# Smaller routing steps on VectorE and 512-column products for the third stage's units, in a two-layer encoder trunk with product-key experts

## The chip, the cores and the metric

The kernel runs on one core of one Trainium2 chip. The metric is the device time of one execution in microseconds (us). The profile names the engines PE (TensorE matmuls), PEld (TensorE weight loads), DVE (VectorE), ACT (ScalarE), POOL (GpSimd) and SP (SyncE, which issues the DMAs).

## The reference, cut to what matters

256 tokens of 1024 features go through two layers. Each layer is an attention (differential in layer 0, stick-breaking in layer 1), a layer norm, a PEER channel mixer and a layer norm. Nearly all of the time is the mixer's:

```python
def _peer(x, w_pq, sub_keys, u, v):              # xt: 256 tokens x 1024
    q = (xt @ w_pq).reshape(T, 8, 2, 64)
    scores = einsum('thcd,hckd->thck', q, sub_keys)        # 8 heads, 2 halves, 128 keys
    s_top, i_top = top_k(scores, 16)
    cand = s_top[:, :, 0, :, None] + s_top[:, :, 1, None, :]
    cand_ids = i_top[:, :, 0, :, None] * 128 + i_top[:, :, 1, None, :]
    g_s, g_i = top_k(cand.reshape(T, 8, 256), 16)
    ids = take_along_axis(cand_ids..., g_i)                # 128 experts a token, of 16384
    gates = softmax(g_s)
    h = gelu(einsum('td,ted->te', x, u[ids]))
    out = einsum('te,ted->td', gates * h, v[ids])
```

## The kernel before, in words

The mixer is dense: the kernel computes h for all 16384 experts and all tokens, sets the gates of experts that a token did not choose to zero, and multiplies by all of v. The experts are cut into 128 *units* of 128 experts, which go in pairs. Products keep fp32 accuracy by splitting both operands: a high half (rounded by ScalarE's copy, `h`, L144) and a low half (the difference `l`, L149, on VectorE, or on GpSimd for the first `N_POOL` = 14 units of a layer). Each product is three matmuls, high x high, high x low and low x high. The activations' two halves are `xh` and `xl` (`xtiles`, L189), 8 rows of 256 tokens each. The buffers of a loaded unit (`raw`, `h`, `l`) rotate over three.

`Hidden.pair` (L807) makes h of a pair: 2 units x 8 rows x 3 matmuls of 256 columns into one PSUM tile `w`, then Gelu on ScalarE (L819). The mixer has three stages.

- First stage: the first `N_STORED` = 42 units. Beside them VectorE does the routing of both token blocks (`routing`, L677): top 16 of 128 keys (`top16`: maxima L705, indices L707, replacement L709, again L712, L714), sums of candidates (L721 to L737), top 16 of those, then indices by masks and folds (L743 to L778), the gates (L780 to L784), four transposes on TensorE, two copies on ScalarE (L791, L792) into `idxT`, and the gates' low half L793. `routing` is a generator; each `yield` claims the microseconds of the work just written down, and `yield None` ends a part. `route_all` (L829) hands out the parts of the two blocks alternately. The loop at L843 adds 0.12 (first 13 units) or 0.072 us of credit per matmul and writes routing steps until the credit is used up, so the claims set where on VectorE the low halves of the units stand between routing steps. VectorE's order is the written order there (`order_r`); the order of the other engines, and where instructions of the next stage are slipped in, is made by a planner that simulates with its own costs.
- Second stage: from `idxT` the gates of 8 tokens at a time, by masks on VectorE (L887 to L904) and products on TensorE (L914, L915), drained onto the stored units (L873, L874); beside it 26 more units (`extra`).
- Third stage: the product with v, two units of v a step, in the order 13 extra pairs, 30 fresh pairs, 21 stored pairs. The fresh pairs' h is made on the way (`make_fresh`, L931): while fresh pairs last, a step holds 48 matmuls of `Hidden.pair` and 24 matmuls of 512 columns with v (`passes`, L199).

Of the kernel before, what the change touches and what calls it, by code (L numbers as in the profile page):

```python
# [10 lines left out]
F32 = mybir.dt.float32  # L11
F32R = mybir.dt.float32r
# [4 lines left out]
AF = mybir.ActivationFunctionType  # L17
OP = mybir.AluOpType
AX = mybir.AxisListType

P = 128
D = 1024
T = 256
NB = 2
DC = 8
# [22 lines left out]
N_POOL = 14  # L48
# [10 lines left out]
def trunk(ctx: ExitStack, tc: tile.TileContext, x, xT, ln_g, ln_b, w_qkv, w_o_a, lam_p, subln, w_kv,  # L59
          w_q, w_o_b, w_pq, sub_k, uT, v, rope, ln_c, out):  # L60
    nc = tc.nc
# [4 lines left out]
    work = ctx.enter_context(tc.tile_pool(name="work", bufs=2))  # L66
    psum = ctx.enter_context(tc.tile_pool(name="psum", bufs=4, space=bass.MemoryType.PSUM))
# [3 lines left out]
    def reg(off, *shape):  # L71
        n = int(np.prod(shape))
        a = big[:, off:off + n]
        if len(shape) == 2:
            return a.rearrange("p (a b) -> p a b", b=shape[1])
        if len(shape) == 3:
            return a.rearrange("p (a b c) -> p a b c", b=shape[1], c=shape[2])
        if len(shape) == 4:
            return a.rearrange("p (a b c d) -> p a b c d", b=shape[1], c=shape[2], d=shape[3])
        return a  # L80
# [106 lines left out]
    units = Units()  # L187

    def xtiles():  # L189
        return (work.tile([P, DC, T], F32R, name="xh", bufs=1), work.tile([P, DC, T], F32R, name="xl", bufs=1))  # L190

    def accs(tag):
        a = [[psum.tile([P, 512], F32, name=tag, tag=tag) for _ in range(NB)] for _ in range(2)]
# [181 lines left out]
    def diff_attention(xh, xl):  # L375
# [161 lines left out]
        for i, _ in enumerate(v_steps(av)):  # L537
# [12 lines left out]
            if i == 7:  # L550
                s2(1)
                s3(1)
        units.later(reg(O_A, NB, D), x)
        oh, ol = xtiles()
        acc = accs("acc")
        wo = moving_steps(acc, oh, ol, lambda d: w_o_a[0, d * P:(d + 1) * P, :], tail=TAIL,
# [13 lines left out]
    def stick_breaking(xh, xl, yv, gb):  # L570
# [60 lines left out]
        for f in range(2):  # L631
            for b in range(NB):
                nc.vector.tensor_copy(V[:, b, f * 512:(f + 1) * 512], av[b][f])
        oh, ol = xtiles()
        acc = accs("acc")
        wo = moving_steps(acc, oh, ol, lambda d: w_o_b[0, d * P:(d + 1) * P, :], tail=TAIL,
# [11 lines left out]
    def peer(layer, xh, xl, spill, o_res):  # L648
# [8 lines left out]
        hx = {}  # L657
# [19 lines left out]
        def routing(b, sc):  # L677
            o = 23552 + b * 4096
            def half(off, *shape):
                n = int(np.prod(shape))  # L680
                return big[:, off:off + n // 2].bitcast(F16).rearrange(
                    "p (a b c) -> p a b c" if len(shape) == 3 else "p (a b) -> p a b",
                    **dict(zip("bc" if len(shape) == 3 else "b", shape[1:])))
# [4 lines left out]
            di = half(o + 584, HP, K, 2)  # L688
# [6 lines left out]
            ef = reg(o + 1576, 3, HP, K)  # L695
# [7 lines left out]
            def top16(lists):  # L703
                for vals, s, i in lists:
                    nc.vector.max(s[:, 0:8], vals)  # L705
                for vals, s, i in lists:
                    nc.vector.max_index(i[:, 0:8], s[:, 0:8], vals)  # L707
                for vals, s, i in lists:
                    nc.vector.match_replace(vals, s[:, 0:8], vals, -3.0e38)  # L709
                yield 0.55 * len(lists)  # L710
                for vals, s, i in lists:
                    nc.vector.max(s[:, 8:16], vals)  # L712
                for vals, s, i in lists:
                    nc.vector.max_index(i[:, 8:16], s[:, 8:16], vals)  # L714
                yield 0.55 * len(lists)

            for l0 in range(0, 2 * HP, 4):
                yield from top16([(sc[:, li, :], s16l[:, li, :], i16l[:, li, :]) for li in range(l0, l0 + 4)])
# [4 lines left out]
            nc.vector.tensor_tensor(di, ia[:, :, 1:K + 1].unsqueeze(3).to_broadcast([P, HP, K, 2]),  # L723
                                    ia[:, :, 0:K].unsqueeze(3).to_broadcast([P, HP, K, 2]), OP.subtract)
            nc.vector.tensor_copy(i2, iu[:, :, 1, :].unsqueeze(3).to_broadcast([P, HP, K, 2]))
            for a0, off, n in SPANS[:8]:
                if a0 in (6, 7):
                    continue
                if a0 == 5:
                    nc.vector.tensor_tensor(  # L730
                        cs[:, :, off:off + 6].rearrange("p h (a b) -> p h a b", b=2),
                        s16[:, :, 0, 5:8].unsqueeze(3).to_broadcast([P, HP, 3, 2]),
                        s16[:, :, 1, 0:2].unsqueeze(2).to_broadcast([P, HP, 3, 2]), OP.add)
                    continue
                nc.vector.tensor_tensor(cs[:, :, off:off + n], s16[:, :, 1, 0:n],
                                        s16[:, :, 0, a0:a0 + 1].to_broadcast([P, HP, n]), OP.add)
            nc.vector.tensor_tensor(cs[:, :, NCAND - 8:NCAND], s16[:, :, 0, 8:16],  # L737
                                    s16[:, :, 1, 0:1].to_broadcast([P, HP, 8]), OP.add)
            yield 2.0
            for h0 in range(0, HP, 4):  # L740
                yield from top16([(cs[:, h, :], g16[:, h, :], p16u[:, h, :]) for h in range(h0, h0 + 4)])
            yield None
# [2 lines left out]
            def fold(dst):  # L745
                w = K // 2
                while w > 1:
                    nc.vector.tensor_tensor(prd[:, :, 0:w, :], prd[:, :, 0:w, :], prd[:, :, w:2 * w, :], OP.add)
                    w //= 2
                nc.vector.tensor_tensor(dst, prd[:, :, 0, :], prd[:, :, 1, :], OP.add)  # L750

            def each(t):
                return t.unsqueeze(1).to_broadcast([P, HP, K, K])

            def times(t):
                nc.vector.tensor_tensor(
                    prd.rearrange("p h a (k t) -> p (h a) k t", t=2), stp.rearrange("p h a (k t) -> p (h a) k t", t=2),
                    t.rearrange("p h a t -> p (h a) t").unsqueeze(2).to_broadcast([P, HP * K, K // 2, 2]), OP.mult)

            nc.vector.tensor_tensor(stp, p16h.unsqueeze(2).to_broadcast([P, HP, K, K]), each(off16), OP.is_ge)  # L760
            nc.vector.tensor_tensor(prd, stp, each(len16), OP.mult)
            yield 2.4
            fold(cc)
            nc.vector.tensor_tensor(cc, p16h, cc, OP.subtract)
            yield 1.6
            times(di)
            fold(ef[:, 0])
            yield 2.6
            nc.vector.tensor_tensor(stp, cc.unsqueeze(2).to_broadcast([P, HP, K, K]), each(row16), OP.is_equal)
            times(i2)  # L770
            fold(ef[:, 1])
            yield 3.8
            ef = ef.rearrange("p c h k -> p c (h k)")
            ei = i16.rearrange("p h c k -> p (h c k)").bitcast(I32).rearrange("p (c n) -> p c n", c=2)
            nc.vector.tensor_copy(ei[:, 1], ef[:, 1])
            nc.vector.tensor_scalar(ei[:, 0], ei[:, 1], 4, None, OP.logical_shift_right)
            nc.vector.tensor_scalar(ei[:, 1], ei[:, 1], 15, None, OP.bitwise_and)
            nc.vector.tensor_copy(ef[:, 1:3], ei)  # L778
            gx = s16.rearrange("p h c k -> p (h c k)")[:, 0:P].rearrange("p (h k) -> p h k", k=K)
            nc.vector.tensor_tensor(gx, g16, g16[:, :, 0:1].to_broadcast([P, HP, K]), OP.subtract)  # L780
            nc.scalar.activation(gx, gx, AF.Exp)
            nc.vector.tensor_reduce(sm[:, 0, :], gx, axis=AX.X, op=OP.add)
            nc.vector.reciprocal(sm[:, 1, :], sm[:, 0, :])
            nc.vector.tensor_tensor(gx, gx, sm[:, 1, :].unsqueeze(2).to_broadcast([P, HP, K]), OP.mult)  # L784
            yield 2.0
            pt = psum.tile([P, 4, P], F32, name="acc", tag="acc")
            for c in range(3):
                nc.tensor.transpose(pt[:, c, :], ef[:, c, :], ident)
# [1 line left out]
            bs = slice(b * P, (b + 1) * P)  # L790
            nc.scalar.activation(idxT[:, 0:3, bs], pt[:, 0:3, :], AF.Copy)  # L791
            nc.scalar.activation(idxT[:, 3, bs], pt[:, 3, :], AF.Copy, scale=GS)  # L792
            nc.vector.scalar_tensor_tensor(idxT[:, 4, bs], pt[:, 3, :], GS, idxT[:, 3, bs], OP.mult, OP.subtract)  # L793
            yield 0.5

        class Hidden:
# [10 lines left out]
            def pair(self, i, dst):  # L807
# [10 lines left out]
                            yield i + k  # L818
                nc.scalar.activation(dst, ps.rearrange("p a b -> p (a b)"), AF.Gelu)  # L819

        hidden = Hidden()

        def slot(i):
            return big[:, i * T:(i + 2) * T]
# [3 lines left out]

        def route_all():  # L829
            rs = [routing(b, sc[b]) for b in range(NB)]  # L830
            for r in rs:
                yield from iter(lambda r=r: next(r), None)
            for r in rs:
                yield from iter(lambda r=r: next(r), None)
            for r in rs:
                yield from r

        side = route_all()
        credit = 0.0
# [2 lines left out]
        hidden.fetch()  # L842
        for i in range(0, N_STORED, 2):  # L843
            for u in hidden.pair(i, slot(i)):
                credit += 0.12 if u + 1 < N_POOL else 0.072
                while credit > 0.0:
                    c = next(side, None)
                    if c is None:
                        credit = -1e9
                        break  # L850
                    credit -= c
# [40 lines left out]
        for t8 in range(0, T, 8):  # L892
            if t8 % (2 * NR) == 0:
                parts(t8)
            rs = slice(t8 // 2 % NR, t8 // 2 % NR + 4)
# [13 lines left out]
            for r in range(2):  # L909
                ps = psum.tile([P, 4, NE], F32, name="acc", tag="acc")  # L910
# [20 lines left out]
        def make_fresh():  # L931
            if fq:
                i = fq.pop(0)
                hx[i] = work.tile([P, 2 * T], F32, name="hx", tag="hw", bufs=RING)
                for _ in hidden.pair(i, hx[i]):
                    pass

        wq = {}

# [28 lines left out]
        for s in range(n + 1):  # L968
            if s >= len(ext) - 2:
                make_fresh()  # L970
            if s >= 1:
                i = order[s - 1]
# [26 lines left out]
    xh, xl = xtiles()  # L999
# [26 lines left out]
    for layer in range(2):  # L1026
        acc = diff_attention(xh, xl) if layer == 0 else stick_breaking(xh, xl, reg(res, NB, D), gb)
        xh, xl = xtiles()
# [5 lines left out]
        if layer == 0:  # L1034
            xh, xl = xtiles()
# [48 lines left out]
```

## Time and profile before

| what | us |
|---|---|
| median of 3 runs (lowest, highest) | 1892.78 (1888.84, 1894.35) |
| the profiled execution, whole | 1894.14 |
| its span, first to last instruction | 1892.3 |

The span of the trace is 1.8 us shorter than the time of the execution that it belongs to. Times in rows are counted from the span's start. Busy times of matmuls overlap, since matmuls are pipelined, so the mean duration of one is longer than the distance between two starts. "Idle before" is the engine's idle time just ahead of an instruction, with what released it.

### The profile page before, as it was taken

What the parts mean: (1) busy time and instruction counts of PE and PEld (TensorE: products, weight loads), DVE (VectorE), ACT (ScalarE), POOL (GpSimd) and SP (SyncE); (2) the same over time, 40 slices, a digit from 0 to 9 for tenths busy, and PEclk for the clock granted to TensorE, in tenths of its full rate; (3) what the DMA queues carried; (4) which work ended last, traced back from release to release, by engine and by line L of the source; (5) the groups of instructions that cost most, each with busy time, mean ns of one, the idle gap of its engine ahead of it and who ended that gap; (6) DMA issues with size and microseconds to landing.
All of it is one profiled execution on the core that took longest, in us unless ns stands there. A gap on an engine that the chain in (4) does not pass through costs nothing.

```text
span 1892.3 us, 30931 instructions
## 1 busy us (share of the span) xinstructions
PE 1831.4 (97%) x12264; PEld 1655.8 (87%) x12264; DVE 1232.2 (65%) x2402; ACT 911.5 (48%) x1244; POOL 176.6 (9%) x190
## 2 busy tenths in 40 slices
PE   8999989999999999999999999899999999999997
PEld 6879989898999999978798799889989999998786
DVE  5666988986555555575553569889865555555655
ACT  4545445545444444454447454454544444445442
POOL 5434200000000000000122251000000000000001
PEclk9989999999999999999999999999999999999999
DMA  6533544335555555575643345443355555555753
GB/s 210 177 134 135 184 136 137 123 124 200 179 200 191 191 186 182 186 266 190 211 152 105 123 157 179 133 146 113 134 202 184 191 181 189 185 191 192 255 190 133
DMA packets 90449, 325.40 MB, mean 172 GB/s; under 512 B 10176, under 2 KB 10560, under 8 KB 89664
## 3 DMA queue, kind: packets, MB, share of 16 engines
q1 hardware_dynamic: 90304, 323.43, 50.4%
q8 instruction: 96, 1.57, 0.3%
q14 instruction: 49, 0.40, 0.1%
HBM read 320.24 MB, written 3.15 MB: 171 GB/s over the span
## 4 chain that ended last, share of the span: by engine, by line
PE 77%; DVE 17%; DMA 2%; issue 2%; ACT 1%; POOL 1%; SPq 0%; POOLq 0%; ACTq 0%; DVEq 0%
PE acc L199 38%; PE w L816 28%; PE acc L244 4%; DVE l L149 3%; DVE gl L900 2%; DVE big L873 2%; DVE gh L900 2%; DVE oa L904 1%; PE w L244 1%; PE acc L444 1%; PE w L199 1%; DVE big L707 1%; DVE big L709 1%; DMA big<-in_ln_g 1%; DVE big L714 1%
## 5 line engine op out<-in xcount | busy, mean ns | idle before, releaser
L144 ACT ACTIVATE h<-raw 128x1024 fp32r<-128x1024 f32 x579 | 606.9, 1059 | 854.7 <-PE acc L199 457.0
L149 DVE TENSOR_TENSOR l<-raw,h 128x1024 fp32r<-128x1024 f32 x526 | 642.8, 1235 | 530.4 <-ACT h L144 530.1
L816 PE MATMUL w<-xh,l 128*128 128x256 f32 x2048 | 580.3, 285 | 15.6 <-DVE l L149 15.6
L816 PE MATMUL w<-xh,h 128*128 128x256 f32 x2048 | 586.6, 287 | 2.1 <-ACT h L144 2.1
L816 PE MATMUL w<-xl,h 128*128 128x256 f32 x2048 | 580.6, 284 | 0.0
L816 PEld LDWEIGHTS w<-xh,l 128*128 128x128 f32 x2048 | 392.8, 192 | 21.6 <-DVE l L149 16.6
L199 PE MATMUL acc<-l,wh 128*128 128x512 f32 x1024 | 399.3, 391 | 2.9 <-DVE l L149 2.9
L816 PEld LDWEIGHTS w<-xh,h 128*128 128x128 f32 x2048 | 393.8, 192 | 7.9 <-ACT h L144 2.5
L199 PE MATMUL acc<-h,wl 128*128 128x512 f32 x1024 | 399.5, 391 | 0.0
L816 PEld LDWEIGHTS w<-xl,h 128*128 128x128 f32 x2048 | 393.7, 192 | 4.8
L199 PE MATMUL acc<-h,wh 128*128 128x512 f32 x1024 | 278.3, 391 | 0.0
L199 PEld LDWEIGHTS acc<-l,wh 128*128 128x128 f32 x1024 | 192.6, 188 | 40.0 <-DVE l L149 3.8
L199 PEld LDWEIGHTS acc<-h,wl 128*128 128x128 f32 x1024 | 192.8, 188 | 36.8
L199 PEld LDWEIGHTS acc<-h,wh 128*128 128x128 f32 x1024 | 188.1, 188 | 35.6
L149 POOL TENSOR_TENSOR l<-raw,h 128x1024 fp32r<-128x1024 f32 x53 | 130.4, 2461 | 178.2 <-ACT h L144 167.4
L959 DVE TENSOR_TENSOR wl<-big,wh 128x512 fp32r<-128x512 f32 x128 | 87.0, 687 | 5.1 <-PE acc L199 4.7
L173 POOL TENSOR_TENSOR ahead<-big,ahead 128x512 fp32r<-128x512 f32 x12 | 16.5, 1403 | 754.2 <-ACT ahead L163 754.2
L958 ACT ACTIVATE wh<-big 128x512 fp32r<-128x512 f32 x128 | 78.2, 620 | 12.1 <-PE acc L199 7.8
L915 PE MATMUL acc<-oa,gl 128*128 128x128 f16 x512 | 66.3, 220 | 14.2 <-DVE gl L900 12.7
L295 POOL TENSOR_TENSOR mv<-mv,mhalf 128x1 f32<-128x1 f32 x8 | 4.8, 600 | 745.1 <-DVE mv L294 745.1
L914 PE MATMUL acc<-oa,gh 128*128 128x128 f16 x512 | 70.6, 220 | 0.0
L874 ACT ACTIVATE big<-acc 128x344 f32<-128x344 f32 x128 | 51.4, 453 | 30.5 <-DVE big L873 30.5
(215 smaller groups left out, 1749.2 us busy)
## 6 DMA issues: line engine op xcount, KB each, us to landing
raw<-in_uT SPq DMA_DIRECT2D x256, 512.0 KB, 3.3
raw<-in_v SPq DMA_DIRECT2D x256, 512.0 KB, 3.6
raw<-in_w_qkv SPq DMA_DIRECT2D x23, 512.0 KB, 3.7
raw<-in_w_kv SPq DMA_DIRECT2D x12, 512.0 KB, 4.0
raw<-in_w_o_a SPq DMA_DIRECT2D x8, 512.0 KB, 4.0
big<-in_w_pq SPq DMA_DIRECT2D x8, 512.0 KB, 6.7
raw<-in_w_pq SPq DMA_DIRECT2D x8, 512.0 KB, 5.0
raw<-in_w_q SPq DMA_DIRECT2D x8, 512.0 KB, 3.8
```

The lines of the kernel that those rows point to most:

```text
L144: self.h = nc.scalar.activation(h, raw, AF.Copy)
L149: o = e.tensor_tensor(l, raw, h.bitcast(F32), OP.subtract)
L199: nc.tensor.matmul(acc[b][f], a[:, d, ts], w[:, fs], start=(first and q == 0), stop=(last and q == 2))
L244: nc.tensor.matmul(acc[n // 2][:, n % 2, :], w[:, c:c + P], a[:, d, :], start=(d == 0 and q == 0 and n % 2 == 0), stop=(d == DC - 1 and q ...
L816: nc.tensor.matmul(ps[:, k, :], w[:, ds], a[:, d, :], start=(d == 0 and q == 0), stop=(d == DC - 1 and q == 2))
L873: nc.vector.scalar_tensor_tensor(wv[:, 0:N_STORED], pv[:, 0:N_STORED], 1.0 / GS, wv[:, 0:N_STORED], OP.mult, OP.mult)
L874: nc.scalar.activation(wv[:, N_STORED:], pv[:, N_STORED:], AF.Copy, scale=1.0 / GS)
L900: nc.vector.tensor_tensor(dst.rearrange("p r (a b) t -> p r a b t", b=16), hi[:, rs].unsqueeze(3).to_broadcast([P, 4, 8, 16, 2]), lo[:, rs ...
L914: nc.tensor.matmul(ps[:, k, :], gh[:, m, :, e], oa[:, m, :, e], start=True, stop=False)
L915: nc.tensor.matmul(ps[:, k, :], oj[:, m, :, e], oa[:, m, :, e], start=False, stop=True)
L958: nc.scalar.activation(wh, s, AF.Copy)
L959: nc.vector.tensor_tensor(wl, s, wh.bitcast(F32), OP.subtract)
```

## The change

Four things change. (1) The two halves of the activations become one tile, `xhl`, in which the rows of high and low half alternate. (2) `top16` and the third part of the routing offer more and smaller steps, with other claims, and the credit per matmul goes from 0.12 to 0.13 and from 0.072 to 0.08. (3) L793 moves behind a `yield None`, and `route_all` has three rounds, so that the L793 of both blocks come after everything else of the routing. (4) `make_fresh` uses a new `wide_pair`: per row the high half of the unit is multiplied with both halves of the activations in one matmul of 512 columns, the low half with the high half of the activations in one of 256 columns; each unit has a PSUM tile of its own, whose two halves VectorE adds into the destination, and Gelu works in place.

```diff
     def xtiles():
-        return (work.tile([P, DC, T], F32R, name="xh", bufs=1), work.tile([P, DC, T], F32R, name="xl", bufs=1))
+        units.both = work.tile([P, DC, 2, T], F32R, name="xhl", bufs=1)
+        return units.both[:, :, 0, :], units.both[:, :, 1, :]
...
             def top16(lists):
                 for vals, s, i in lists:
                     nc.vector.max(s[:, 0:8], vals)
+                yield 0.2 * len(lists)
                 for vals, s, i in lists:
                     nc.vector.max_index(i[:, 0:8], s[:, 0:8], vals)
+                yield 0.26 * len(lists)
                 for vals, s, i in lists:
                     nc.vector.match_replace(vals, s[:, 0:8], vals, -3.0e38)
-                yield 0.55 * len(lists)
+                yield 0.26 * len(lists)
                 for vals, s, i in lists:
                     nc.vector.max(s[:, 8:16], vals)
+                yield 0.2 * len(lists)
                 for vals, s, i in lists:
                     nc.vector.max_index(i[:, 8:16], s[:, 8:16], vals)
-                yield 0.55 * len(lists)
+                yield 0.26 * len(lists)
...
             nc.vector.tensor_copy(i2, iu[:, :, 1, :].unsqueeze(3).to_broadcast([P, HP, K, 2]))
+            yield 1.2
...
-            yield 2.0
+            yield 1.2
...
             nc.vector.tensor_tensor(stp, p16h.unsqueeze(2).to_broadcast([P, HP, K, K]), each(off16), OP.is_ge)
+            yield 1.3
             nc.vector.tensor_tensor(prd, stp, each(len16), OP.mult)
-            yield 2.4
+            yield 1.2
             fold(cc)
             nc.vector.tensor_tensor(cc, p16h, cc, OP.subtract)
+            yield 1.8
+            times(di)
+            yield 1.2
+            fold(ef[:, 0])
             yield 1.6
-            times(di)
-            fold(ef[:, 0])
-            yield 2.6
             nc.vector.tensor_tensor(stp, cc.unsqueeze(2).to_broadcast([P, HP, K, K]), each(row16), OP.is_equal)
+            yield 1.2
             times(i2)
+            yield 1.2
             fold(ef[:, 1])
-            yield 3.8
+            yield 1.6
...
             nc.vector.tensor_copy(ef[:, 1:3], ei)
+            yield 0.9
...
             nc.vector.tensor_tensor(gx, gx, sm[:, 1, :].unsqueeze(2).to_broadcast([P, HP, K]), OP.mult)
-            yield 2.0
+            yield 0.8
...
             nc.scalar.activation(idxT[:, 3, bs], pt[:, 3, :], AF.Copy, scale=GS)
+            yield None
             nc.vector.scalar_tensor_tensor(idxT[:, 4, bs], pt[:, 3, :], GS, idxT[:, 3, bs], OP.mult, OP.subtract)
             yield 0.5
...
+            def wide_pair(self, dst):
+                for k in range(2):
+                    if len(self.got) < 2:
+                        self.fetch()
+                    h, l = self.got.pop(0)
+                    ps = psum.tile([P, 2 * T], F32, name="w", tag="w")
+                    for d in range(DC):
+                        ds = slice(d * P, (d + 1) * P)
+                        nc.tensor.matmul(ps, h[:, ds], both[:, d].rearrange("p c t -> p (c t)"), start=(d == 0),
+                                         stop=False, skip_group_check=True)
+                        nc.tensor.matmul(ps[:, 0:T], l[:, ds], xh[:, d, :], start=False, stop=(d == DC - 1),
+                                         skip_group_check=True)
+                    nc.vector.tensor_reduce(dst[:, k * T:(k + 1) * T], ps.rearrange("p (c t) -> p t c", t=T), axis=AX.X, op=OP.add)
+                nc.scalar.activation(dst, dst, AF.Gelu)
...
         def route_all():
             rs = [routing(b, sc[b]) for b in range(NB)]
-            for r in rs:
-                yield from iter(lambda r=r: next(r), None)
-            for r in rs:
-                yield from iter(lambda r=r: next(r), None)
+            for _ in range(3):
+                for r in rs:
+                    yield from iter(lambda r=r: next(r), None)
             for r in rs:
                 yield from r
...
-                credit += 0.12 if u + 1 < N_POOL else 0.072
+                credit += 0.13 if u + 1 < N_POOL else 0.08
...
-                for _ in hidden.pair(i, hx[i]):
-                    pass
+                hidden.wide_pair(hx[i])
```

## Rows read from the trace of the kernel before

**Rows 1.** The page, part 1: busy us (share of the span) xinstructions of each engine

```profile
PE 1831.4 (97%) x12264; PEld 1655.8 (87%) x12264; DVE 1232.2 (65%) x2402; ACT 911.5 (48%) x1244; POOL 176.6 (9%) x190
```

**Rows 2.** Table by stretches of layer 0's mixer: length, PE PEld DVE ACT POOL busy, PEclk, DMA

```profile
172.00:209.00 37.00, 35.93 (x300) 35.73 (x298) 36.93 (x255) 18.28 (x21) 24.07 (x10) 1.00 0.41 143
209.00:250.00 41.00, 40.71 (x339) 40.71 (x340) 37.31 (x149) 17.09 (x21) 0.00 (x0) 1.00 0.54 183
...
266.20:282.00 15.80, 9.37 (x64) 9.35 (x64) 15.38 (x26) 3.83 (x6) 0.00 (x0) 0.78 0.29 93
282.00:302.00 20.00, 20.00 (x171) 19.88 (x170) 12.88 (x22) 11.23 (x14) 0.00 (x0) 1.00 0.53 172
302.00:420.00 118.00, 110.89 (x1141) 107.13 (x1140) 113.89 (x249) 60.36 (x106) 0.00 (x0) 1.00 0.35 121
...
475.00:806.00 331.00, 331.00 (x2122) 301.74 (x2121) 176.56 (x176) 151.91 (x178) 0.00 (x0) 1.00 0.56 188
```

**Rows 3.** The list of waits, whole span: us in total, times, longest

```profile
PE w L816 <- DVE l L149: 15.6, 4, 6.4
...
DVE hi L887 <- ACT idxT L791: 11.0, 2, 5.5
```

**Rows 4.** Timeline of PE: start, us, instruction [idle before <-releaser]

```profile
209.29 0.39 PE L816 MATMUL w<-xh,l 128*128 128x256 f32 x1 [1.36 <-DVE l L149]
...
272.64 0.58 PE L816 MATMUL w<-xh,l 128*128 128x256 f32 x1 [6.43 <-DVE l L149]
```

**Rows 5.** Timeline of DVE in layer 0's first stage

```profile
208.02 2.35 DVE L149 TENSOR_TENSOR l<-raw,h 128x1024 fp32r<-128x1024 f32 x2
...
237.38 0.22 DVE L743 CAST big<-big 128x128 f16<-128x128 uint32 x1
...
258.85 0.28 DVE L782 TENSOR_REDUCE big<-big 128x8 f32<-128x128 f32 x1 [1.62 <-ACT big L781]
...
259.62 1.22 DVE L149 TENSOR_TENSOR l<-raw,h 128x1024 fp32r<-128x1024 f32 x1
266.35 0.23 DVE L887 TENSOR_TENSOR hi<-iota,idxT 128x128 f16<-128x128 f16 x1 [5.51 <-ACT idxT L791]
...
271.37 2.36 DVE L149 TENSOR_TENSOR l<-raw,h 128x1024 fp32r<-128x1024 f32 x2
273.64 1.48 DVE L748 TENSOR_TENSOR big<-big 128x1024 f16<-128x1024 f16 x3
...
295.11 0.29 DVE L793 SCALAR_TENSOR_TENSOR idxT<-acc,idxT 128x128 f16<-128x128 f32 x1 [3.31 <-ACT idxT L792]
```

**Rows 6.** Timeline of ACT ahead of block 0's copies

```profile
262.96 1.06 ACT L144 ACTIVATE h<-raw 128x1024 fp32r<-128x1024 f32 x1 [2.03 <-PE w L816]
...
265.83 0.48 ACT L791 ACTIVATE idxT<-acc 128x384 f16<-128x384 f32 x1
```

**Rows 7.** The chain that ended last, in order of time: start, us, what

```profile
272.64 8.47 PE w L816 x48
...
426.15 48.99 PE acc L199 x216
475.14 3.59 PE w L816 x30
486.03 3.47 PE w L816 x29
...
497.28 3.47 PE w L816 x29
...
1213.86 7.36 PE w L816 x48
```

**Rows 8.** Groups of instructions, shapes apart: busy us, mean ns | idle before

```profile
L816 PE MATMUL w<-xh,h 128*128 128x256 f32 x2048 | 586.6, 287 | 2.1 <-ACT h L144 2.1
...
L819 ACT ACTIVATE hx<-w 128x512 f32<-128x512 f32 x86 | 49.9, 581 | 0.0
...
L470 DVE TENSOR_REDUCE big<-w 128x2 f32<-128x512 f32 x8 | 5.4, 688 | 4.0 <-PE w L468 4.0
```

More of the change, by code (lines that the diff above doesn't have):

```diff
@@ L819, in pair @@
                 nc.scalar.activation(dst, ps.rearrange("p a b -> p (a b)"), AF.Gelu)
+            def wide_pair(self, dst):
[12 more added lines that the diff above has]
+                nc.scalar.activation(dst, dst, AF.Gelu)
+        both = units.both
         hidden = Hidden()
```

## The prediction

> **What bounds the kernel now.** I read the page first, then the table by stretches, the list of waits, and at the stalls the timelines of TensorE, VectorE and ScalarE. TensorE has work over 97% of the span [rows 1], so a gain must be fewer TensorE cycles or one of its few gaps. The stretches of the first layer show which stage has what [rows 2]. In the third stage (475 to 806 us: 30 pairs of fresh units, each beside two units of v) TensorE is busy throughout and VectorE little more than half of it, so only TensorE's own time counts there. In the first stage it is the other way round: VectorE has 36.93 of 37 us at 172 to 209, and at 266 to 282 TensorE works 9.4 of 15.8 us with its clock granted at 0.78 on the mean, between its levels of 1.2 and 2.4 GHz. The second stage (302 to 420) has VectorE at 97%, and the diff does not touch it. The second layer repeats the pattern.
>
> The list of waits names the gaps of the first stage: TensorE waits for a unit's low half (L149 on VectorE) four times, 15.6 us [rows 3]. The first layer has one of 1.36 and one of 6.43 us [rows 4], and 2 x 7.79 = 15.6 makes the second layer's the same. How the long one comes about stands in the two timelines. VectorE ends block 0's gates, does one low half at 259.62, and then idles 5.51 us until ScalarE's copy L791 [rows 5]; that copy runs at 265.83, behind a split that began at 262.96 [rows 6]. L793, next in VectorE's written order, needs the copy's successor L792, so VectorE has to idle there; L887 of the second stage was merely slipped in front of it. The next low halves stand behind this and start at 271.37, and TensorE resumes at 272.64. The clock is low afterwards: 48 matmuls take 8.47 us there and 7.36 us in the second layer [rows 7], against 48 x 0.1197 = 5.75 us in the third stage (30 of them in 3.59 us) [rows 7].
>
> **Third stage, TensorE.** A unit has 24 matmuls of 256 columns now, and 8 of 512 and 8 of 256 after: the same columns in a third fewer instructions. Matmuls overlap, so their mean duration is no price; the chain gives start to start. A 256-column one costs 0.1197 us (3.59/30), a 512-column one with a new weight each time 0.2268 us (48.99/216) [rows 7]. Now: 24 x 0.1197 = 2.873. After: 8 x 0.2268 + 8 x 0.1197 = 2.772. That is 0.101 us a unit. The period confirms the prices: 48 x 0.1197 + 24 x 0.2268 = 11.19, and 497.28 - 486.03 = 11.25 us [rows 7]. Fresh units: 128 - 42 - 26 = 60 a layer, 120 in all, hence **-12.1 us**. The bounds are 0, should the excess over the columns not be one per instruction, and -12.1.
>
> The Trainium skill's page "TensorE: Matmul & The Clock Gate", section "Back-to-back issue gap", speaks against this size: it gives the warm isolated gap as N/2.4 plus about 2.5 ns, so that by it (an estimate) 8 matmuls fewer save 8 x 2.5 = 20 ns a unit and 2.4 us in all, not 12.1. The trace does not agree: 119.7 and 226.8 ns lie 13 ns above what that page's N/2.4 gives.
>
> **Third stage, VectorE and ScalarE.** Added are 2 reductions a pair, 120 in all, that read 128x512 out of PSUM. The nearest row is a reduction of that size from PSUM, 0.688 us [rows 8]; its output is narrower and its stride shorter, so the bounds are 0.69 and twice that. I take 0.69: 120 x 0.69 = 83 us of VectorE. It is costed at nothing because of idle time: 176.6 + 41 of 331 us [rows 2] is 66%. What stands behind a reduction is the next low halves. Three buffers rotate, so the unit three ahead gets its high half when TensorE has ended unit k: 1.06 us on ScalarE, 1.14 on VectorE and some 0.3 of hand-over make it ready 2.5 us after, and it is needed two units later, 2 x 2.87 + 0.24 = 6.0 us. The slack is 3.5 us. A reduction of unit k also waits for the end of unit k, so even one queued ahead of that low half takes 0.7 of the 3.5. Without that cover each would cost up to 0.69, 83 us in all. Gelu stays one instruction of 0.58 us [rows 8], now in place; the product that needs it comes two steps of 11 us later. PSUM tiles go from one to two a pair out of four: the pair after next finds its tiles free a whole step earlier. DMA issues keep their number and order.
>
> **Layout of the two halves.** Each row of a half stays contiguous; only the step between rows doubles. I take 0. If the shared tile made a reader of the high half wait for the low half, the first product after each of three layer norms would be some 1 us late, 3 us in all.
>
> **Routing.** Removed: VectorE's wait for L792 between block 0's gates and block 1's third part. With L793 behind both blocks, VectorE goes straight on to block 1, some 23 us of work, while the transposes and copies pass. Block 1's own wait (3.31 us at 295.11 [rows 5]) stays, with L793 of block 0 ahead of it. Gone with the stall: 2 x 6.43 + (8.47 - 5.75) + (7.36 - 5.75) = 17.2 us. Gone too, the 1.36 us twice (2.7): the low half at 208.02 stands behind a whole half list of the candidates [rows 5]. By the new steps, 13 units x 24 x 0.13 = 40.6 us of claims are handed out before it, which end after the first four maxima of that list (37.8 for both blocks' first part, then 1.2, 1.2, 0.8). Some 1.4 us of index and replace steps move behind it. Sum 19.9 us.
>
> What is late next: the new claims are handed out faster, 0.08 x 24 = 1.92 us a unit against 1.73, and one low half of 1.14 goes with each. A block's third part takes 259.62 - 237.38 = 22.2 us less six low halves (6.8), so 15.4 us, of which 1.62 is waiting for Exp [rows 5] (a low half is 1.14 start to start: two take 271.37 to 273.64); it claims 12.8 and so is spread over 6.67 units. VectorE needs 15.4 + 6.67 x 1.14 = 23.0 us for what TensorE eats in 6.67 x 2.87 = 19.1, and falls 3.9 us behind per block, 7.8 per layer, against the slack of 3.5: TensorE waits 4.3. (Before, 12.4 claimed at 1.73: 3.0 behind per block.) Bounds: 0, and 7.6 if block 1's 3.31 comes on top. The same sum of before gives block 1 a lag of 3.0 + 3.3 over 3.5, and TensorE is busy 20.00 of 20 us there [rows 2]; so it overstates, and I take 3 us a layer, in pieces too short to lower the clock (after the wait of 1.36 us it stayed at 1.00 [rows 2, 4]). **Routing: -19.9 + 6 = -14 us.** Does the second stage keep it? Its drains need all stored units, so it starts when the first stage ends on TensorE; its first sets (some 3 us of VectorE), now done in the stall, must fit into the first stage's last units, where VectorE works 12.88 of 20 us [rows 2]. They fit.
>
> **Sum.** The profiled execution took 1894.14 us (span 1892.3), 1.4 above the median of the three runs. 1894.1 - 12.1 - 14 = 1868.0, and on the median's footing **1867 us**.
>
> **Rivals.** *Another wait takes the stall's place*: the planner slips L887 or L889 in front of block 1's steps again, where they wait for block 0's copies, or the lag of 7.8 comes out in full with a low clock behind it. For it: VectorE is FIFO, and the 5.51 us were put down to L887. Against it: that idling needed L793 next in line. The routing then brings 2 us or so: 1894.1 - 12.1 - 2, 1879 on the median's footing. *A larger gain*: no lag shows at all, 1861. *The wide form saves little*, because the 13 ns hang on something else than the number of instructions: 1879 by the routing's 14 us alone. Against it: both widths show the same excess. *Slower*: the planner puts a unit's reduction ahead of the low half that TensorE needs for the very next unit. Then that low half starts only after the end of the unit before, TensorE idles 0.69 + 1.14 = 1.8 us, and all 120 times this is 220 us. It decides from 26/120 = 0.22 us a unit, or one unit in eight so queued: 1900 and more. Against it: in the third stage VectorE idles for ScalarE's split, so low halves are queued well ahead. *It does not do what it says*: the planner works from its own costs; if new orders cost in other places what is won here, the time stays within 0.3%, 1887 to 1898.
>
> **How the numbers follow.** Both parts as summed, with 0 to 7.6 us of lag a layer, 0.62 (1861 to 1876); another wait (1879) 0.16; the wide form saves little 0.10; no change 0.06; slower 0.06. I count the gain without lag into the first. 0.3% of 1893 us is 5.7 us, about what a measurement of this kernel can tell from no change (the three runs lie 5.5 apart). Faster by more than that: 0.62 + 0.16 + 0.10 = 0.88. The range goes from 1858 (no lag, and the 2.1 us in which the first stage waits for ScalarE's high half [rows 8] gone as well) to 1881 (one of the two parts wholly lost), and leaves out the last two cases and some of the edges.
>
> **What would show it.** Matmuls fall by 960 to 11304, with 960 of 512 columns into w. The period of the third stage falls from 11.25 to 11.05 us with TensorE still busy all through. 120 reductions near 0.69 us stand on VectorE; waits of TensorE for them or for low halves there would refute the cover. The wait of L887 for L791 is gone, TensorE's waits for L149 in the first stage fall from 15.6 to about 6 us, none over 3, and the granted clock is 1.00 at 260 to 285. The prediction is wrong if a wait of 5 us stays in the first stage, if a 512-column product into w costs more than 0.24 us, or if the second stage grows by what the first gave.

## The result and the profile after

The changed kernel takes 1870.88 us (median; 1868.66 to 1874.6), the kernel before beside it 1890.81. The ratio is 0.990, with a 95% interval of 0.9883 to 0.9917: faster by 19.9 us. The prediction was 1867 us with a range of 1858 to 1881.

The page of the changed kernel, part 1, answers to [rows 1]:

```profile
PE 1818.9 (97%) x11304; PEld 1598.8 (86%) x11304; DVE 1311.6 (70%) x2522; ACT 920.4 (49%) x1244; POOL 176.6 (9%) x190
```

960 matmuls are gone, and VectorE has 79 us more to do. The table by stretches, in the columns of [rows 2]; the first two lines are the end of layer 0's first stage, where the stall was, the third is the third stage:

```profile
246.00:262.50 16.50, 13.82 (x115) 13.39 (x113) 12.48 (x28) 9.69 (x12) 0.00 (x0) 1.00 0.39 125
262.50:277.00 14.50, 14.50 (x120) 14.41 (x121) 12.26 (x20) 6.42 (x7) 0.00 (x0) 1.00 0.58 180
...
464.00:800.00 336.00, 336.00 (x1688) 283.55 (x1687) 223.16 (x244) 162.00 (x186) 0.00 (x0) 1.00 0.63 191
```

The clock stays at 1.00 where it was 0.78, and TensorE is still busy all through the third stage, with VectorE at 66%. The list of waits of the changed kernel, answering to [rows 3] (us in total, times, longest):

```profile
DVE hx L844 <- PE w L842: 38.7, 84, 0.7
...
DVE big L792 <- ACT big L791: 9.9, 4, 2.7
...
PE w L827 <- DVE l L149: 5.5, 5, 2.2
```

TensorE's waits for low halves fell from 15.6 to 5.5 us. The reductions (L844) wait for TensorE, not TensorE for them. Where the time of the two profiled executions went is read best from the chain in order of time (start, us, what) at the same places of the program. Of the kernel before:

```profile
138.47 23.04 PE acc L244 x192
...
406.86 3.88 PE w L816 x32
...
1079.07 23.67 PE acc L244 x192
...
1347.23 3.88 PE w L816 x32
```

Of the changed kernel, where L245 is L244 and L827 is L816:

```profile
134.51 23.04 PE acc L245 x192
...
395.90 3.88 PE w L827 x32
...
470.33 2.78 PE acc L200 x12
...
473.45 1.84 PE acc L200 x8
...
478.33 0.94 PE acc L200 x4
...
481.82 4.56 PE acc L200 x20
...
490.96 0.93 PE acc L200 x4
...
492.58 2.78 PE acc L200 x12
...
781.87 2.78 PE acc L200 x12
...
1064.82 23.81 PE acc L245 x192
...
1326.87 3.88 PE w L827 x32
```

From the query product (first place) to a place late in the second stage (second place) the kernel before takes 268.4 us in layer 0 and 268.2 in layer 1, the changed one 261.4 and 262.1: the routing gave 7.0 + 6.1 = 13.1 us. Two steps of the third stage take 492.58 - 470.33 = 22.25 us, and the 28 steps up to 781.87 take 311.54 us, so one takes 11.126 us for 11.25 [rows 7]; 60 steps save 7.4 us.

The spans differ by 24.3 us, and 3.96 of these lie ahead of the first place (138.47 and 134.51). Most of these come from the granted clock there, not from the change. The table by stretches for layer 0's attention, first of the kernel before:

```profile
86.00:91.00 5.00, 5.00 (x25) 4.58 (x26) 3.46 (x9) 3.38 (x14) 0.00 (x0) 0.61 0.55 193
91.00:101.00 10.00, 10.00 (x49) 8.43 (x48) 5.47 (x18) 4.95 (x21) 1.03 (x1) 0.50 0.00 0
101.00:112.00 11.00, 10.83 (x69) 10.09 (x68) 7.66 (x24) 5.46 (x14) 4.45 (x50) 0.85 0.15 50
```

and of the changed one:

```profile
86.00:91.00 5.00, 5.00 (x33) 4.57 (x33) 3.81 (x10) 2.85 (x11) 0.00 (x0) 0.66 0.48 135
91.00:101.00 10.00, 10.00 (x55) 9.14 (x55) 7.46 (x25) 6.57 (x28) 3.46 (x49) 0.66 0.01 2
101.00:112.00 11.00, 10.83 (x71) 9.39 (x69) 6.05 (x17) 5.37 (x9) 4.20 (x4) 1.00 0.17 48
```

With levels of 1.0 and 0.5 of the full clock (2.4 and 1.2 GHz) the first had 5 x 0.78 + 10 + 11 x 0.3 = 17 us at the low clock, the second 5 x 0.68 + 10 x 0.68 = 10; 7 us at half speed are 3.5 us. Of the change, only the layout of the activations reaches this stretch. With the layout edit alone (below) the profiled execution had 1.00, 0.83 and 1.00 there and a span of 1886.7 us, while the median was that of the kernel before. So medians are compared below, and within traces only the same stretches.

### The profile page after: what moved, and what is told of

Read it like the earlier page. It is cut to its first block, busy times and chain, and to the rows that moved or that the text cites. A ratio compares the mean times of both kernels' runs of the same rounds, so it can differ in the third digit from the quotient of the medians.

```text
span 1868.0 us, 29132 instructions
## 1 busy us (share of the span) xinstructions
PE 1818.9 (97%) x11304; PEld 1598.8 (86%) x11304; DVE 1311.6 (70%) x2522; ACT 920.4 (49%) x1244; POOL 176.6 (9%) x190
## 4 chain that ended last, share of the span: by engine, by line
PE 80%; DVE 13%; issue 2%; DMA 2%; ACT 2%; POOL 1%; SPq 0%; ACTq 0%; POOLq 0%; DVEq 0%
PE acc L200 38%; PE w L827 12%; PE w L840 12%; PE w L842 6%; PE acc L245 4%; DVE l L149 4%; DVE gl L926 2%; DVE big L899 2%; DVE gh L926 2%; PE w L245 1%; DVE oa L930 1%; PE w L200 1%; PE acc L445 1%; DMA big<-in_ln_g 1%; ACT h L144 1%
## 5 line engine op out<-in xcount | busy, mean ns | idle before, releaser
L144 ACT ACTIVATE h<-raw 128x1024 fp32r<-128x1024 f32 x579 | 613.5, 1060 | 821.9 <-PE acc L200 333.7
L827 PE MATMUL w<-xhl,h 128*128 128x256 f32 x2176 | 400.0, 286 | 0.3 <-ACT h L144 0.2
L840 PE MATMUL w<-xhl,h 128*128 128x512 f32 x960 | 340.0, 396 | 0.0
L827 PEld LDWEIGHTS w<-xhl,h 128*128 128x128 f32 x2176 | 338.1, 192 | 0.9 <-ACT h L144 0.7
L827 PE MATMUL w<-xhl,l 128*128 128x256 f32 x1088 | 308.3, 285 | 5.7 <-DVE l L149 5.5
L842 PE MATMUL w<-xhl,l 128*128 128x256 f32 x960 | 268.8, 280 | 0.0
L840 PEld LDWEIGHTS w<-xhl,h 128*128 128x128 f32 x960 | 180.5, 188 | 42.5
L827 PEld LDWEIGHTS w<-xhl,l 128*128 128x128 f32 x1088 | 208.1, 192 | 7.6 <-DVE l L149 6.9
L842 PEld LDWEIGHTS w<-xhl,l 128*128 128x128 f32 x960 | 181.2, 189 | 6.2
L844 DVE TENSOR_REDUCE hx<-w 128x256 f32<-128x512 f32 x120 | 82.7, 690 | 38.9 <-PE w L842 38.7
L200 PE MATMUL acc<-h,xhl 128*128 128x512 f32 x256 | 84.2, 403 | 6.2 <-ACT h L132 4.8
L983 ACT ACTIVATE wh<-big 128x512 fp32r<-128x512 f32 x128 | 77.7, 616 | 15.6 <-PE acc L200 11.1
```

The source lines that it names most:

```text
L144: self.h = nc.scalar.activation(h, raw, AF.Copy)
L200: nc.tensor.matmul(acc[b][f], a[:, d, ts], w[:, fs], start=(first and q == 0), stop=(last and q == 2))
L827: nc.tensor.matmul(ps[:, k, :], w[:, ds], a[:, d, :], start=(d == 0 and q == 0), stop=(d == DC - 1 and q == 2))
L840: nc.tensor.matmul(ps, h[:, ds], both[:, d].rearrange("p c t -> p (c t)"), start=(d == 0), stop=False, skip_group_check=True)
L842: nc.tensor.matmul(ps[:, 0:T], l[:, ds], xh[:, d, :], start=False, stop=(d == DC - 1), skip_group_check=True)
L844: nc.vector.tensor_reduce(dst[:, k * T:(k + 1) * T], ps.rearrange("p (c t) -> p t c", t=T), axis=AX.X, op=OP.add)
```

## The experiments

The change was cut into its parts. Each run is given with its median and the ratio to the kernel before (median 1890.25 for the first four, 1889.7 for the next four, 1891.14 for the last two).

**L793 moved, alone.** Claims, steps and credits as before:

```diff
             nc.scalar.activation(idxT[:, 3, bs], pt[:, 3, :], AF.Copy, scale=GS)
+            yield None
             nc.vector.scalar_tensor_tensor(idxT[:, 4, bs], pt[:, 3, :], GS, idxT[:, 3, bs], OP.mult, OP.subtract)
...
-            for r in rs:
-                yield from iter(lambda r=r: next(r), None)
-            for r in rs:
-                yield from iter(lambda r=r: next(r), None)
+            for _ in range(3):
+                for r in rs:
+                    yield from iter(lambda r=r: next(r), None)
```

> The kernel before with L793 moved behind both blocks alone; claims, steps and credits as before. Theory (the stall was VectorE's wait for L792): the wait of 5.5 us and the stall of 6.43 us are gone, the waits of 1.36 us stay; the lag per block is the old 3.0 us, 6.0 for two against 3.5 of slack, so at most 2.5 us of waits come in: 11 to 15 us below the kernel before. Rival (the coarse steps made the stall): under 4 us below, with a wait of 4 us or more left.

1877.58 us, ratio 0.9928 (0.9915 to 0.9941): 12.7 us below. Its list of waits:

```profile
DVE hi L887 <- ACT idxT L791: 3.4, 2, 1.7
...
PE w L817 <- DVE l L149: 6.5, 7, 1.4
```

No wait for a low half is over 1.4 us. One moved line does what the whole routing part does. L887 is still slipped in, but costs 1.7 us and not 5.5.

**Smaller steps and new credits, alone.** The routing's edits and both credits, with L793 left where it was (the inverse of the diff above, on the changed routing):

> The kernel before with the smaller steps and the new credits alone; L793 stays behind each block's copies. Theory: the waits of 1.36 us go, the stall of 6.43 us stays or grows by the faster claims (3.9 us of lag per block for 3.0): between 3 us below the kernel before and 2 above. Rival (the coarse steps made the stall): 10 us or more below.

1890.76 us, ratio 1.0002 (0.9993 to 1.0011): nothing. Its list of waits shows the stall, now 5.7 us long. The wait of 1.36 us is gone from layer 0, but a new one of 2.94 us stands at 290.79, behind block 1's gates:

```profile
PE w L825 <- DVE l L149: 16.9, 4, 5.7
...
DVE hi L896 <- ACT idxT L800: 10.7, 2, 5.3
```

**The whole routing part, alone.** The changed kernel with `xtiles` and `make_fresh` as before:

> The kernel before with the routing's part of the change alone (steps, credits, L793 behind both blocks); third stage as before. Theory: 13 us below the kernel before, first stages 6 to 7 us shorter per layer, TensorE's waits for low halves about 3 us per layer. Rival (the wide form won 12): 8 us below.

1877.35 us, ratio 0.9933 (0.9919 to 0.9946): 12.9 us below, as with L793 alone. TensorE waits 5.3 us for low halves, longest 2.2.

**The wide form, alone.** The kernel before with `xhl` and `wide_pair`:

```diff
-                for _ in hidden.pair(i, hx[i]):
-                    pass
+                hidden.wide_pair(hx[i])
```

> The kernel before with the shared tile and wide_pair alone; the routing is as before. Theory (the wide form won 7.1 us, because 512 and 256 columns in turn cost 234 + 116 = 350 ns and not the 346.5 of the prediction): 7 us below the kernel before, and the stall of 6.43 us per layer still there. Rival (the wide form won the predicted 12 us, and the routing less): 12 us below. Rival (layout or planner give something of their own ahead of the mixer): 11 us below, with the attention shorter at the same clock.

1882.68 us, ratio 0.9960 (0.9947 to 0.9972): 7.6 us below, which excludes the 12 us of the rival (the interval is 5 to 10 us). The waits of the first stage are those of before (15.9 us, longest 6.4). The parts add: 12.9 + 7.6 = 20.5, and both together gave 19.9.

**The layout, alone.** Only `xtiles` changed:

> The kernel before with the shared tile alone, no other edit. Theory: no difference within 2 us. Rival (a reader of the high half waits for the low half, or the other step between rows costs something): 3 us or more above; or below, if the 4 us that the profiled executions differ by ahead of the first mixer are the layout's.

1889.86 us, ratio 0.9997 (0.9988 to 1.0006). The layout costs and gives nothing that can be measured.

**Each reduction twice.**

```diff
-                    nc.vector.tensor_reduce(dst[:, k * T:(k + 1) * T], ps.rearrange("p (c t) -> p t c", t=T), axis=AX.X, op=OP.add)
+                    for _ in range(2):
+                        nc.vector.tensor_reduce(dst[:, k * T:(k + 1) * T], ps.rearrange("p (c t) -> p t c", t=T), axis=AX.X, op=OP.add)
```

> The changed kernel with each of the 120 reductions done twice (same values). Theory (VectorE's idle time covers them): 83 us more of VectorE and the time within 2 us of the changed kernel, no wait of TensorE in the third stage. Rival (a reduction holds up the next low halves): 10 us or more above it.

1869.70 us, 1.2 below the changed kernel's median and within its runs. Its group of reductions (shapes, count | busy us, mean ns | idle before) and the table's line of the third stage:

```profile
L845 DVE TENSOR_REDUCE hx<-w 128x256 f32<-128x512 f32 x240 | 164.7, 687 | 36.2 <-PE w L842 35.2
```

```profile
464.00:800.00 336.00, 336.00 (x1688) 283.49 (x1687) 253.70 (x302) 162.65 (x186) 0.00 (x0) 1.00 0.61 191
```

82 us more of VectorE in all, 76% of it used in the third stage, and TensorE has no gap. The cover is real, and it holds for twice the load.

**The second credit back to 0.072.**

```diff
-                credit += 0.13 if u + 1 < N_POOL else 0.08
+                credit += 0.13 if u + 1 < N_POOL else 0.072
```

> The changed kernel with the second credit back from 0.08 to 0.072. Theory (the lag of VectorE behind the faster claims makes the remaining waits): a block's third part claims 12.8 at 1.73 us a unit, 7.41 units, 15.4 + 7.41 x 1.14 = 23.8 us of VectorE for 21.3 of TensorE, 2.5 us of lag for 3.9; the waits for low halves fall from 2.7 us per layer to under 1, and the time by 2 to 4 us. Rival (the end of the routing decides): the routing ends 4 units later, the second stage starts late, 0 to 6 us above the changed kernel.

1868.28 us, ratio 0.9890 (0.9875 to 0.9905), an interval that overlaps the changed kernel's. The theory fell: the waits for low halves did not shrink. The median is 2.6 us lower, which is what the theory forecast, but by luck: the waits that it spoke of stayed. The timeline of TensorE in layer 0's first stage, first of the changed kernel ([idle before <-releaser]):

```profile
256.90 0.39 PE L827 MATMUL w<-xhl,l 128*128 128x256 f32 x1 [0.47 <-DVE l L149]
...
262.48 0.39 PE L827 MATMUL w<-xhl,l 128*128 128x256 f32 x1 [2.21 <-DVE l L149]
...
278.34 0.33 PE L799 MATMUL acc<-ident,big 128*128 128x128 f32 x1 [0.98 <-DVE big L794]
```

and with the lower credit:

```profile
262.48 0.39 PE L827 MATMUL w<-xhl,l 128*128 128x256 f32 x1 [0.47 <-DVE l L149]
...
268.05 0.39 PE L827 MATMUL w<-xhl,l 128*128 128x256 f32 x1 [2.20 <-DVE l L149]
```

The same two waits, 5.6 us later. What made them stands in VectorE's timeline of the changed kernel:

```profile
250.53 0.29 DVE L790 TENSOR_TENSOR big<-big 128x128 f32<-128x128 f32 x1
253.46 0.28 DVE L792 TENSOR_REDUCE big<-big 128x8 f32<-128x128 f32 x1 [2.65 <-ACT big L791]
...
259.66 0.23 DVE L913 TENSOR_TENSOR hi<-iota,idxT 128x128 f16<-128x128 f16 x1 [0.96 <-ACT idxT L801]
...
261.20 1.22 DVE L149 TENSOR_TENSOR l<-raw,h 128x1024 fp32r<-128x1024 f32 x1
```

Two waits for ScalarE stand ahead of the late low half: 2.65 us for the Exp of block 0's gates, and 0.96 us for the copy L801, in front of an instruction of the second stage that the planner put between two folds. ScalarE's timeline shows what each waited behind:

```profile
251.82 1.28 ACT L791 ACT_TABLE_LOAD   x1
...
257.36 1.28 ACT L830 ACT_TABLE_LOAD   x1
...
259.15 0.48 ACT L801 ACTIVATE idxT<-acc 128x384 f16<-128x384 f32 x1
```

An ACT_TABLE_LOAD of 1.28 us stands directly ahead of the Exp (L791), and another ahead of the Gelu (L830) behind which the copy runs. That these two waits make the low half late is read from the order of the rows; no run took one of them away. The claims are not wholly without a part: the wait for the Exp was 1.62 us before [rows 5] and is 3.62 us with the lower credit. What the lower credit did remove is TensorE's wait of 0.98 us for the gates ahead of block 1's transposes. From the first to the second place of the chain, layer 0 takes 260.0 us with it for 261.4.

**512s first, then 256s.**

```diff
                     for d in range(DC):
                         ds = slice(d * P, (d + 1) * P)
                         nc.tensor.matmul(ps, h[:, ds], both[:, d].rearrange("p c t -> p (c t)"), start=(d == 0),
                                          stop=False, skip_group_check=True)
+                    for d in range(DC):
+                        ds = slice(d * P, (d + 1) * P)
                         nc.tensor.matmul(ps[:, 0:T], l[:, ds], xh[:, d, :], start=False, stop=(d == DC - 1),
                                          skip_group_check=True)
```

> The changed kernel, with wide_pair's eight products of 512 columns first and its eight of 256 after them. Theory (a 512 next to a 256 costs 3.8 ns more than the two cost among their own kind): 8 x 226.7 + 8 x 119.6 = 2.77 us a unit for 2.80, so 3.6 to 4.4 us below the changed kernel. Rival (the 512-column product into w is dear in itself, at 234 ns): no difference, and adjacent ones keep 234 ns.

1865.39 us, ratio 0.9868 (0.9853 to 0.9884): 5.5 us below the changed kernel's median, with intervals that barely touch. Its chain in order of time, in the third stage:

```profile
470.76 4.56 PE acc L200 x20
...
475.56 1.84 PE w L840 x8
477.40 0.95 PE w L844 x8
...
479.96 0.91 PE acc L200 x4
...
481.93 4.56 PE acc L200 x20
...
493.10 4.56 PE acc L200 x20
...
503.88 4.56 PE acc L200 x20
```

Three steps take 503.88 - 470.76 = 33.12 us, one 11.04 for 11.126: 60 x 0.086 = 5.2 us. The products with v take 4.56 + 0.91 us of each step here, 0.228 us each; the rest, (33.12 - 16.41)/48, is 0.348 us for a pair of a 512 and a 256. In the changed kernel two steps hold 2.78 + 1.84 + 0.94 + 4.56 + 0.93 = 11.05 us of products with v, 0.2302 each and up to 0.2317 (2.78/12), and (22.25 - 11.05)/32 = 0.350 us remain for a pair. So about 1.8 us of the 5.2 are in the units and about 3.3 in the products with v. The theory had the sign and nearly the size, but only a third of it in the place that it named. The rival (the 512s dear in themselves at 234 ns) fell: next to each other they cost 0.230 us (1.84/8).

**Both of these, and the least that does it.** The first joins the grouping and the lower credit. The second is the kernel before with L793 moved and the grouped `wide_pair`, and with the old steps, claims and credits.

> The changed kernel with wide_pair's products grouped (512s first) and the second credit at 0.072. Theory (the two gains lie in different stages and add): 1870.9 - 5.5 - 2.6 = 1863 us. Rival (the later end of the routing costs what the grouping gives): 1865 or more.

1861.88 us, ratio 0.9846 (0.9833 to 0.9859), the fastest here: 9.0 us below the changed kernel's median. The two gains add.

> The kernel before with only L793 moved and wide_pair grouped; steps, claims and credits as before. Theory (the smaller steps carried nothing): 12.7 + 7.6 + 5.5 us below the kernel before's 1890, that is 1864 us. Rival (the smaller steps are worth what they claim): 1868 or more, since the waits of 1.36 us stay.

1866.53 us, ratio 0.9872 (0.9856 to 0.9887). Beside the grouped kernel with the small steps (0.9868) there is no difference that these runs resolve, though the small waits for low halves stay (7.0 us, longest 1.4). That does not make the small steps worthless. The run before this one has them and the same second credit, and it is 4.7 us faster by the medians (the intervals just touch); from the first to the second place its layer 0 takes 260.25 us and this one's 261.83. It seems that the small steps gain some us at a second credit of 0.072 and that the faster credit gives them away. The two kernels differ in the first credit as well (0.13 and 0.12), and no run parts the two.

## Why the prediction was right, point by point

- *The stall is VectorE's wait for L792, and moving L793 removes it*: right, and shown: the moved line alone gives 12.7 us, the steps without it 0. The routing was to give 14 us and gave 12.9 alone and 13.1 within the two traces. The prediction put the copy L791 behind a split; the rows between show a table load and a Gelu as well, which took 1.8 of the 2.9 us from the start of that split to the copy:

```profile
264.04 1.28 ACT L819 ACT_TABLE_LOAD   x1
265.34 0.60 ACT L819 ACTIVATE big<-w 128x512 f32<-128x512 f32 x1
```

- *What is late next*: the size held (3 us a layer taken; 2.7 and 2.8 measured in the waits for low halves), the reason did not. The step that failed is that VectorE, through the faster claims, "falls 3.9 us behind per block" and that this makes the waits. Slower claims left them as they were, 2.20 us for 2.21. Ahead of the late low half stand VectorE's waits for the Exp and, before a slipped-in instruction, for the copy, 2.65 + 0.96 us; of the first the prediction had counted 1.62 in its sum. So the 3 us were right partly by luck: the sum gave 4.3, and was lowered to 3 because the same sum overstated the waits of before. The rival "another wait takes the stall's place" thus came true in small: L913, the old L887, waits 0.96 us there.
- *The waits of 1.36 us go with the smaller steps*: they did go (the 5.5 us left lie elsewhere), but the saving does not show in the time at the credit of the change: the steps alone, and the least version beside the grouped one, make no difference that can be measured. I had counted 2.7 us for them. At the slower credit some of it seems to show (the last two runs).
- *Third stage, TensorE*: the mechanism was right, the term mis-sized: -12.1 predicted, -7.6 measured alone, -7.4 by the period. A gain of 26 us was predicted and one of 19.9 measured; some 4.6 of the 6.2 us between them are here and 1 is in the routing. That the times, 1867 and 1871, lie only 4 us apart is luck: the median of the kernel before, from which the prediction starts, is 1892.78 over its three runs and 1890.81 over the four beside the changed kernel. The price of the 512-column product came from a stretch where only such products run, 0.2268 us, and it is dearer in the third stage: there the pair of a 512 and a 256 costs 0.350 us and not 0.3465. The trace of before already had a nearer row: its third stage spends 2.75 us on 12 products with v, 0.229 each:

```profile
492.45 2.75 PE acc L199 x12
```

With that, 16 x 0.1197 - 8 x 0.229 = 0.083 us a unit and 10.0 us in all; the last 2.5 are open: they go with products of two widths in turn, but grouping these gave back only some 1.8 in the units.

The estimate of 2.4 us by the formula for an isolated matmul (the Trainium skill, "TensorE: Matmul & The Clock Gate", "Back-to-back issue gap") does not fit this stream of matmuls: the measured 7.6 lies three times above it.

- *Cover for the reductions, layout, ScalarE*: right. 120 reductions of 0.690 us were predicted at 0.688; twice as many cost nothing; the layout alone costs nothing.
- *The slower rival* (a reduction ahead of the next low half) did not occur: no wait of TensorE lies in the third stage.

## What to carry to other kernels

When an in-order engine idles for a copy that another engine makes late, look for the one instruction in its written order that needs it, and move that behind work that is ready; how finely the rest is cut mattered less here (nothing at the faster credit, perhaps some us at the slower one). Look also at what the late engine did just before: here a table load of 1.28 us stood ahead of the late copy and of the late Exp. Price an instruction from the stretch in which it will run, beside the neighbours that it will have: the same 512-column product cost 0.2268 us in one stage and 0.228 to 0.232 in another. And test a cover by doubling what it hides.

## What the runs showed of the hardware that was not expected

- Matmuls of 512 and of 256 columns in turn cost 350 ns a pair; with the eight 512s of a unit together, the step of the third stage fell from 11.126 to 11.04 us, some two thirds of it in the neighbouring products with v (0.2302 to 0.228 us each, 24 a step: 0.055 us). That run changes nothing but the order of TensorE's products, so this part hangs on the order. Why a 512-column product costs 0.2268 us in one stretch and 0.228 in another even so, at a granted clock of 1.00 in both, is open; no run here took the third stage's other traffic away.
- The granted clock in layer 0's attention is low for 10 us in one execution and 17 in another, worth 3.5 us, in a part where the change touches only the layout of the activations, which alone made no difference to the median.
- ScalarE spent 1.28 us on an ACT_TABLE_LOAD each time it went from Gelu to the Exp of the gates and back, and in the first stage VectorE's waits stand behind these.
